# A decoder layer in split fp32: key/value steps two later, one query tile one later, a copy on another engine, last blocks scaled in twos

## The chip, the cores and the metric

The kernel runs on one core of one Trainium2 chip. The metric is the device time of one execution, in microseconds (us). Engines are named as the profile names them: PE is TensorE (PEld its weight loads), DVE is VectorE, ACT is ScalarE, POOL is GpSimd, SP is SyncE, which here only issues DMAs.

## What is computed

One inference step of one layer of a hybrid decoder, in fp32, on 256 prompt positions and 8 sample tokens (264 columns in all) of width 2048:

```python
def trunk_layer(x, attend, shift0, wkv0, lp):
    ...
    x = x + FFN_RES * swiglu(rmsnorm(x, n1), f1g, f1u, f1d)
    h = rmsnorm(x, nm)
    proj = h @ w_in
    ...
    o_att, k_buf, v_buf = attend(q, k, v, sinks)
    o_rwkv, shift, S = rwkv_time_mix(proj[..., ATT_COLS:], shift0, wkv0, mu, w0, w2, a0, a2, g2,
                                     k_k, k_a, r_k, ln_w, ln_b)
    mixed = jnp.concatenate([o_att, o_rwkv.astype(o_att.dtype)], axis=-1)
    x = x + mixed @ w_out
    x = x + FFN_RES * swiglu(rmsnorm(x, n2), f2g, f2u, f2d)
    return x, k_buf, v_buf, S, shift
```

`attend` is attention over a window of 128 positions with sinks and a relative bias (16 query heads in 8 tiles of two, 4 key/value heads in 2 tiles of two); `rwkv_time_mix` is a recurrence with a matrix state for each of 16 heads (8 pairs). A last rmsnorm follows. The new keys, values, states and shift columns are outputs too.

## The kernel before

**Matrix products.** Every weight is read once from memory, in chunks of up to four 128x128 tiles (`raw`, L140, issued by SP). ScalarE casts a chunk to a reduced type (`hi`, L141), and VectorE takes the rest of it (`lo` = raw − hi, through the helper at L68). The activations are split likewise. A product of one tile is three matmuls of 264 columns (hi·hi, hi·lo, lo·hi) through the helper at L84, into an accumulator `acc` in PSUM, of which there are three. A chunk is thus 12 matmuls. In this text they are the projection matmuls, or the big stream.

**Stages.** The first feed-forward part ends near 757 us of the span, mixing (input projection, attention, recurrence, output projection) near 1150, the second feed-forward part near 1921, and the final norm, scaling and stores near 1933.

**Order of work in mixing.** The tiles of the input projection come in the order of `SEQ` (L49). Between the chunks of the projection, everything else is done by generators: after each chunk, `tick` advances each of them by one `yield`, so one step is about one chunk long. `pause(n)` yields n times. They share five PSUM buffers `m`, handed out by `mp()`. A scheduler then sets the final order of the instructions on each engine. The generators are:
- `prep`, once for a pair of recurrent heads. Among other things it transposes (L521, L528), copies the results out (L524 `kr`, L531 and L533 `BT`, the latter two half copies of 64x256 on ScalarE), and does small matmuls XD,ld and uv,gm at L84, whose results ScalarE copies at L544 and L546.
- `chain`, once for each of the four batches of two pairs. It holds the triangular inverse on VectorE (many small `st` and `Xt`), then the tiles `PT`, `kr` and `N` (VectorE, L68), then three state steps: matmuls N,PT and N,kr, then `S` (VectorE, L71), then matmuls S,PT and S,kr, and so on.
- `kvtask`, once for each of two key and two value tiles. It issues the stores out_kp or out_vp from ScalarE's queue (L750) and copies the sample columns into `dkv` on GpSimd (L751), yields once, then transposes dkv (L755) and for value tiles the tile (L758), and copies on ScalarE (L760, L763); L765 stores.
- `attend`, once for each of eight query tiles. Scores (two kv,o tiles, matmuls at L84), addition of the bias and row maximum on VectorE (L801), softmax (exponentials on ScalarE, L78; sums, reciprocal and scaling on VectorE, L68, L776, L75), a pause of `PW[4]` = 9 steps, six transposes (L808 to L810), copies out on ScalarE (L811) and VectorE (L812), then the product with the values (t,kv) and a copy.

**The end.** The last norm's sums and the turning of four of the sixteen output blocks (128x264 each) are done by TensorE (L1045, L1049). The turned part goes out in three stores of 96, 96 and 72 rows: block 0 is scaled on ScalarE and stored by SP (L1066), block 1 is scaled on VectorE and stored by SP (L1069), block 2 is scaled on ScalarE and stored by ScalarE (L1073). Between them ScalarE copies the scale row for GpSimd (L1070). The other twelve blocks are scaled in place and stored by a loop (L1074 to L1078): the first by VectorE and SP, the next three by VectorE and ScalarE's queue, four by GpSimd and SP, four by VectorE and ScalarE's queue.

## Time and profile before

| what | value |
|---|---|
| median of three runs | 1935.79 us (1936.81, 1935.79, 1934.95) |
| profiled execution | 1934.77 us, of it 1932.9 us span |
| mean granted TensorE clock | 0.998 |
| memory read and written | 346.67 MB and 9.69 MB, 184 GB/s over the span |
| ScalarE, VectorE busy | 53%, 68% |

The page of the profile lists how long each engine is busy, the chain of work that ended last, and groups of instructions by line, operation and tile (`out<-in`, shape, count, then busy us and mean ns, then idle time ahead of them and who ended it). The waits of an engine are listed by waiting line and releaser: total us, how many, the longest. A timeline row is start, duration, engine, line, operation, tiles, shape and count; in brackets the idle time ahead and its releaser. On TensorE matmuls overlap, so its pace is read from one start to the next, and not from durations. Times in such rows are us from the start of the span.

### The profile page before, as it was taken

What the parts mean: (1) busy time and instruction counts of PE and PEld (TensorE: products, weight loads), DVE (VectorE), ACT (ScalarE), POOL (GpSimd) and SP (SyncE); (2) the same over time, 40 slices, a digit from 0 to 9 for tenths busy, and PEclk for the clock granted to TensorE, in tenths of its full rate; (3) what the DMA queues carried; (4) which work ended last, traced back from release to release, by engine and by line L of the source; (5) the groups of instructions that cost most, each with busy time, mean ns of one, the idle gap of its engine ahead of it and who ended that gap; (6) DMA issues with size and microseconds to landing.
All of it is one profiled execution on the core that took longest, in us unless ns stands there. A gap on an engine that the chain in (4) does not pass through costs nothing.

```text
span 1932.9 us, 45519 instructions
## 1 busy us (share of the span) xinstructions
PE 1919.4 (99%) x17171; PEld 1897.1 (98%) x17171; DVE 1311.8 (68%) x2606; ACT 1023.7 (53%) x2034; POOL 260.1 (13%) x376
## 2 busy tenths in 40 slices
PE   9999999999999999999999999999999999999998
PEld 9999999999999999999989999999999999999998
DVE  5865555655556568889988977866666666666665
ACT  5644444444444457675657555644444444444446
POOL 0401101011010113222102100300101001010012
PEclk9999999999999999999999999999999999999999
DMA  7666666666666668555646656666666666666664
GB/s 241 178 192 196 185 195 195 183 192 177 190 183 180 188 181 238 177 165 153 176 120 165 210 155 183 175 188 188 189 195 195 186 192 189 194 195 184 193 181 150
DMA packets 218464, 357.27 MB, mean 185 GB/s; under 512 B 33516, under 2 KB 71804, under 8 KB 218244
## 3 DMA queue, kind: packets, MB, share of 16 engines
q1 hardware_dynamic: 211936, 346.02, 60.8%
q10 hardware_dynamic: 6308, 8.35, 1.4%
q8 instruction: 134, 2.20, 0.4%
q14 instruction: 86, 0.70, 0.1%
HBM read 346.67 MB, written 9.69 MB: 184 GB/s over the span
## 4 chain that ended last, share of the span: by engine, by line
PE 96%; DVE 1%; ACT 1%; issue 1%; DMA 0%; POOLq 0%; POOL 0%; ACTq 0%; DVEq 0%
PE acc L84 89%; PE m L84 6%; DVE lo L68 0%; ACT t L78 0%; ACT hi L141 0%; DMA x<-in_x 0%; DVE t L801 0%; DVE st L68 0%; DVE Xt L68 0%; DMA ld<-in_bias 0%; ACT BT L533 0%; ACT L78 0%; POOLq L1187 0%; DVE PT L68 0%; PE m L528 0%
## 5 line engine op out<-in xcount | busy, mean ns | idle before, releaser
L68 DVE TENSOR_TENSOR lo<-raw,hi 128x512 fp32r<-128x512 f32 (+1 forms) x1288 | 874.0, 682 | 510.4 <-ACT hi L141 486.9
L141 ACT CAST hi<-raw 128x512 fp32r<-128x512 f32 (+1 forms) x1288 | 776.8, 606 | 820.2 <-PE acc L84 745.2
L84 PE MATMUL acc<-x,hi 128*128 128x264 f32 x4840 | 893.4, 286 | 0.8 <-ACT hi L141 0.8
L84 PEld LDWEIGHTS acc<-x,hi 128*128 128x128 f32 x4840 | 750.1, 189 | 4.3 <-ACT hi L141 1.0
L84 PE MATMUL acc<-x,lo 128*128 128x264 f32 x2420 | 691.3, 286 | 0.2 <-DVE lo L68 0.2
L84 PE MATMUL acc<-h,hi 128*128 128x264 f32 x2752 | 495.0, 284 | 0.0
L84 PEld LDWEIGHTS acc<-x,lo 128*128 128x128 f32 x2420 | 457.2, 189 | 2.7 <-issue 0.7
L84 PEld LDWEIGHTS acc<-h,hi 128*128 128x128 f32 x2752 | 424.4, 189 | 0.0
L84 PE MATMUL acc<-h,lo 128*128 128x264 f32 x1376 | 387.8, 284 | 0.0
L84 PEld LDWEIGHTS acc<-h,lo 128*128 128x128 f32 x1376 | 259.2, 189 | 0.0
L68 POOL TENSOR_TENSOR t<-t,t 128x264 f32<-128x264 f32 x74 | 79.8, 1078 | 1096.1 <-DVE t L68 949.8
L84 PE MATMUL acc<-y,hi 128*128 128x264 f32 x648 | 122.7, 284 | 0.0
L84 PE MATMUL acc<-o,hi 128*128 128x264 f32 x648 | 120.1, 284 | 0.0
L84 PE MATMUL acc<-kv,hi 128*128 128x264 f32 x582 | 109.8, 285 | 0.0
L84 PEld LDWEIGHTS acc<-y,hi 128*128 128x128 f32 x648 | 101.2, 189 | 0.1
L84 PEld LDWEIGHTS acc<-o,hi 128*128 128x128 f32 x648 | 100.1, 189 | 0.0
L71 DVE SCALAR_TENSOR_TENSOR x<-acc,x 128x264 f32<-128x264 f32 (+1 forms) x193 | 81.1, 425 | 24.3 <-PE acc L84 23.4
L84 PE MATMUL acc<-y,lo 128*128 128x264 f32 x324 | 92.0, 284 | 0.0
L84 PE MATMUL acc<-o,lo 128*128 128x264 f32 x324 | 92.0, 284 | 0.0
L84 PEld LDWEIGHTS acc<-kv,hi 128*128 128x128 f32 x582 | 89.9, 189 | 0.2
L68 DVE TENSOR_TENSOR t<-acc,t 128x264 f32<-128x264 f32 x156 | 67.4, 432 | 32.9 <-PE acc L84 32.9
L84 PE MATMUL acc<-kv,lo 128*128 128x264 f32 x291 | 82.9, 285 | 0.0
(307 smaller groups left out, 1592.5 us busy)
## 6 DMA issues: line engine op xcount, KB each, us to landing
raw<-in_gu SPq DMA_DIRECT2D x688, 256.0 KB, 3.4
raw<-in_dn SPq DMA_DIRECT2D x224, 256.0 KB, 2.9
raw<-in_win SPq DMA_DIRECT2D x152, 256.0 KB, 3.4
raw<-in_dn SPq DMA_DIRECT2D x160, 192.0 KB, 2.8
raw<-in_wout SPq DMA_DIRECT2D x64, 256.0 KB, 3.5
xsp<-x ACTq DMA_DIRECT2D x16, 132.0 KB, 3.4
x<-xsp SPq DMA_DIRECT2D x16, 132.0 KB, 4.2
ld<-in_sT SPq DMA_DIRECT2D x16, 128.0 KB, 3.6
```

The costliest lines, as they stand in the source:

```text
L68: return e.tensor_tensor(out=out, in0=a, in1=b, op=op)
L71: return V.scalar_tensor_tensor(out=out, in0=a, scalar=s, in1=b, op0=op0, op1=op1)
L84: return TE.matmul(out, lhsT, rhs, start=start, stop=stop, **k)
L141: A.copy(hi[:, :w], raw[:, :w])
```

## The change

- Key and value tiles: the one `yield` ahead of the transposes becomes `pause(KVW)` with KVW = 3.
- First query tile (`t` = 0): the pause between softmax and transposes becomes 10 steps instead of 9.
- In the last batch, the second of the two half copies into `BT` runs on VectorE instead of ScalarE (for each of its two pairs).
- The turned block 1 is stored from ScalarE's queue instead of SP's.
- Of the first four blocks of the last loop, SP now stores two and ScalarE's queue two, instead of one and three.

One line is inserted near the top, so line numbers behind L43 are one higher after the change.

```diff
+KVW = 3
...
                 for h in range(2):
-                    A.copy(BT[HALF[h], :, HALF[1]], bp[HALF[1 - h], :, HALF[1]])
+                    (V.tensor_copy if h and bt.i == len(BATCH) - 1 else A.copy)(BT[HALF[h], :, HALF[1]], bp[HALF[1 - h], :, HALF[1]])
...
                     G.tensor_copy(dkv[r, w, p, :], xs[h % len(xs)][r, NP:T])
-                yield
+                yield from pause(KVW)
...
-                yield from pause(PW[4])
+                yield from pause(PW[4] + (not t))
...
                 ts(V, y, x, r, ALU.mult)
-                SP.dma_start(o, y)
+                A.dma_start(o, y)
...
-                for e, q, o, n, r in ((V, SP, 0, 1, rp[:, :T]), (V, A, 1, 3, rp[:, :T]), (G, SP, 4, 4, rb), (V, A, 12, 4, rp[:, :T])):
+                for e, q, o, n, r in ((V, SP, 0, 2, rp[:, :T]), (V, A, 2, 2, rp[:, :T]), (G, SP, 4, 4, rb), (V, A, 12, 4, rp[:, :T])):
```

The scheduler's order moves with it, at more places than the edited ones. In the rows below, names with a number are tiles (the number tells tiles of one name apart), and a count stands at the end.

TensorE around the transposes of the first value tile, in the middle of the input projection (`bk` feeds the `BT` copies, XD,ld and uv,gm are `prep`'s small matmuls). Before, from the transposes of bk, and at the end of the small matmuls:

```order
L84 MATMUL acc_13622<-x_107,hi_13666 128x264 x2
L528 MATMUL m_13334<-C,bk_13035 128x128 x4
L84 MATMUL m_13399<-XD,ld_13268 64x2
...
L84 MATMUL m_13429<-uv_11864,gm_13272 64x64
L755 MATMUL m_13492<-C,dkv 8x128
L758 MATMUL m_13492<-C,t_13370 128x128 x2
```

The same places after:

```order
L529 MATMUL m_13330<-C,bk_13035 128x128 x4
L756 MATMUL m_13366<-C,dkv 8x128
L85 MATMUL acc_13622<-x_107,hi_13666 128x264 x2
L85 MATMUL acc_13622<-x_107,lo_13667 128x264
L85 MATMUL acc_13622<-x_107,hi_13666 128x264
L85 MATMUL m_13399<-XD,ld_13268 64x2
...
L85 MATMUL m_13429<-uv_11864,gm_13272 64x64
L756 MATMUL m_13528<-C,dkv 8x128
L759 MATMUL m_13528<-C,t_13370 128x128 x2
```

A key tile's transpose (m_13366) and projection matmuls now stand between the transposes of bk and the small matmuls; the value tile's transposes still follow the latter.

TensorE around the first query tile's transposes, behind `chain`'s matmuls m_14099 for the second batch. Before:

```order
L84 MATMUL m_14099<-uv_11129,gm_12243 64x64
L808 MATMUL m_14142<-C,t_13690 128x128
L809 MATMUL m_14142<-C,t_13689 128x128
...
L808 MATMUL m_14148<-C,t_13692 128x128
...
L84 MATMUL acc_14157<-x_106,hi_14159 128x264 x2
...
L84 MATMUL m_14176<-N_13888,PT_13393 64x64
```

After:

```order
L85 MATMUL m_14099<-uv_11129,gm_12243 64x64
L85 MATMUL acc_14145<-x_106,hi_14147 128x264 x2
...
L85 MATMUL acc_14145<-x_108,lo_14287 128x264
L85 MATMUL m_14164<-N_13888,PT_13393 64x64
...
L809 MATMUL m_14185<-C,t_13690 128x128
L810 MATMUL m_14185<-C,t_13689 128x128
...
L809 MATMUL m_14191<-C,t_13692 128x128
```

The six transposes have moved behind the matmuls with N; ahead of those stand 18 projection matmuls instead of the transposes and 23.

VectorE at the same place, before:

```order
L68 TENSOR_TENSOR PT_13393<-m_14068,C 64x384
L776 RECIPROCAL stb_14008<-stb_14008 128x4
L68 TENSOR_TENSOR PT_13393<-m_14068,C 64x384
L68 TENSOR_TENSOR kr_11703<-m_14069,kr_11703 128x192
L68 TENSOR_TENSOR lo_14326<-raw_14324,hi_14325 128x512
L68 TENSOR_TENSOR st_14047<-X_13482,Xt_13483 128x64
L68 TENSOR_TENSOR kr_12042<-m_14069,kr_12042 128x192
L75 TENSOR_SCALAR t_13998<-t_13998,stb_14008 128x256
L75 TENSOR_SCALAR t_13999<-t_13999,stb_14008 128x128
L68 TENSOR_TENSOR N_13888<-m_14098,wc 128x512
```

After:

```order
L69 TENSOR_TENSOR PT_13393<-m_14068,C 64x384
L69 TENSOR_TENSOR lo_14326<-raw_14324,hi_14325 128x512
L76 TENSOR_SCALAR t_13998<-t_13998,stb_14008 128x256
L76 TENSOR_SCALAR t_13999<-t_13999,stb_14008 128x128
L69 TENSOR_TENSOR st_14047<-X_13482,Xt_13483 128x64
L69 TENSOR_TENSOR PT_13393<-m_14068,C 64x384
L69 TENSOR_TENSOR kr_11703<-m_14069,kr_11703 128x192
L69 TENSOR_TENSOR kr_12042<-m_14069,kr_12042 128x192
L69 TENSOR_TENSOR N_13888<-m_14098,wc 128x512
```

Between the first PT and N stand the same instructions in another order, without the reciprocal.

## The prediction

> **What bounds the kernel now.** I read the page first: what share of the span each engine is busy, the chain that ended last, and the two costliest groups of the engines beside TensorE.

> ```profile
> span 1932.9 us, 45519 instructions
> ...
> PE 1919.4 (99%) x17171; PEld 1897.1 (98%) x17171; DVE 1311.8 (68%) x2606; ACT 1023.7 (53%) x2034; POOL 260.1 (13%) x376
> ...
> PE 96%; DVE 1%; ACT 1%; issue 1%; DMA 0%; POOLq 0%; POOL 0%; ACTq 0%; DVEq 0%
> ...
> L68 DVE TENSOR_TENSOR lo<-raw,hi 128x512 fp32r<-128x512 f32 (+1 forms) x1288 | 874.0, 682 | 510.4 <-ACT hi L141 486.9
> L141 ACT CAST hi<-raw 128x512 fp32r<-128x512 f32 (+1 forms) x1288 | 776.8, 606 | 820.2 <-PE acc L84 745.2
> ```

> TensorE is the bound: busy for 1919.4 of 1932.9 us. The change takes no matmul away. So it can win only in the 13.5 us in which TensorE is not busy, in the dead time where its two streams meet, and behind its last matmul. Next, TensorE's waits over the whole span, cut to those whose neighbourhood the change moves, and the mixing stage that holds them (columns: stretch, its length, busy PE, PEld, DVE, ACT, POOL, granted clock, DMA share, GB/s):

> ```profile
> PE m L808 <- DVE PT L68: 1.2, 1, 1.2
> ...
> PE m L755 <- issue: 0.7, 1, 0.7
> PE m L84 <- ACT BT L533: 0.4, 1, 0.4
> ...
> PE m L84 <- ACT kr L544: 0.2, 1, 0.2
> ```

> ```profile
> 760.00:1150.00 390.00, 386.97 (x4432) 366.58 (x4431) 334.15 (x924) 246.12 (x627) 68.76 (x167) 1.00 0.58 167
> ```

> These are 2.5 us. In the whole mixing stage TensorE is without work for 390 − 387 = 3.0 us, VectorE is busy for 334 of 390 (86%), and the clock is full. So the ceiling of the three mixing edits is about 3 us plus dead time between streams. Of 1935.79 us, 0.2% is 3.87 us; that is about what a measurement of this kernel can tell from no change. The profiled execution took 1934.77 us (1.9 us lie around its span), 1.0 below the median of the runs: I sum against the profile and carry the difference over to the median.

> **Key and value tiles two steps later.** First TensorE's rows where the transposes of a value tile stood, then ScalarE's:

> ```profile
> 939.05 0.25 PE L84 MATMUL m<-XD,ld 64*64 64x2 f32 x2
> ...
> 940.05 0.27 PE L755 MATMUL m<-C,dkv 128*8 128x128 f32 x1 [0.74 <-issue]
> ```

> ```profile
> 937.08 1.07 ACT L524 COPY kr<-m 64x128 f32<-64x128 f32 x4
> ...
> 939.20 0.74 ACT L533 COPY BT<-m 64x256 f32<-64x256 f32 x2
> ```

> L755 found no free PSUM buffer until ScalarE's L533 copies ended at 939.94; that is the 0.74 us. In the new order the value tile's transposes still stand right behind the XD,ld and uv,gm matmuls, and take a buffer that a small L763 copy (764 now) has freed meanwhile. But the second half of those small matmuls now takes the buffer of the L533 copies. Counted from the four transposes that feed these copies, ScalarE still has by my estimate some half of a cast (0.35 of 0.61, the page's row above) to do, two kr copies (0.54), and the half copies, 0.37 + 0.74: 2.0 us. TensorE has one transpose (0.1), four projection matmuls (0.5) and the first half of the small ones (0.9, an estimate: sixteen uv,gm alone take 0.68 in a row below, and as many XD,ld go between): 1.5. So 0.5 of waiting comes where 0.74 went: −0.25; ends −0.74 (the copies are done in time) and +0.4 (all of their 1.1 us is waited for). The two out_kp/out_vp stores and GpSimd's copies of a kv tile stand ahead of the pause; of the later kvn stores nobody waits.

> **First query tile one step later.** TensorE, then VectorE, where the wait of 1.19 us lies:

> ```profile
> 964.25 0.33 PE L808 MATMUL m<-C,t 128*128 128x128 f32 x1
> ...
> 965.98 0.30 PE L808 MATMUL m<-C,t 128*128 128x128 f32 x1 [1.19 <-DVE PT L68]
> ...
> 966.26 0.49 PE L84 MATMUL acc<-x,hi 128*128 128x264 f32 x2
> 966.59 0.28 PE L84 MATMUL acc<-x,lo 128*128 128x264 f32 x1
> 966.71 0.40 PE L84 MATMUL acc<-x,hi 128*128 128x264 f32 x2
> 966.94 0.28 PE L84 MATMUL acc<-x,lo 128*128 128x264 f32 x1
> ...
> 968.89 0.41 PE L84 MATMUL acc<-x,hi 128*128 128x264 f32 x2
> 969.23 0.27 PE L84 MATMUL m<-N,PT 64*64 64x64 f32 x1
> ```

> ```profile
> 964.61 0.56 DVE L68 TENSOR_TENSOR PT<-m,C 64x384 f32<-64x384 f32 x1
> ...
> 965.28 0.55 DVE L68 TENSOR_TENSOR PT<-m,C 64x384 f32<-64x384 f32 x1
> ...
> 966.14 0.68 DVE L68 TENSOR_TENSOR lo<-raw,hi 128x512 fp32r<-128x512 f32 x1
> ...
> 967.60 0.68 DVE L68 TENSOR_TENSOR N<-m,wc 128x512 f32<-128x512 f32 x1
> ...
> 970.90 0.47 DVE L71 SCALAR_TENSOR_TENSOR S<-m,wc,N 128x64 f32<-128x64 f32 x2
> ...
> 974.24 0.47 DVE L71 SCALAR_TENSOR_TENSOR S<-m,wc,N 128x64 f32<-128x64 f32 x2
> ```

> Before, six transposes come first, the second three wait for the buffer that PT frees, then 23 projection matmuls, then N,PT. After, 18 projection matmuls come first, then N,PT, then the transposes, which wait no more. The pace of projection matmuls is (966.94 − 966.59)/3 = 0.117 us. So TensorE, free at 964.25, reaches N,PT at 964.25 + 18 × 0.117 + 0.2 for two changes of stream = 966.55. VectorE is the one that is late: between the first PT and N the new order has the same instructions, only shuffled (the lo and the softmax scalings now ahead of the second PT) and without the reciprocal that lay between the two PT (some 0.1 us). So N ends near 967.60 + 0.68 − 0.1 = 968.2: **a new wait of 1.6 us at N,PT takes the place of the 1.19**. Behind N,PT still come the six transposes (twice 966.26 − 965.98, 0.56), five projection matmuls (0.6) and 0.1 of changing, so the place that was reached at 969.23 is reached at 969.45: +0.2. The next state step S has two lo ahead of it instead of one (+0.68) and lacks two copies: VectorE is there at about 970.8, TensorE at 971.5, no wait. The second S follows 3.3 us later on VectorE (974.24 − 970.90), so ends near 974.5, 3.0 after TensorE's 971.5. TensorE has 7 projection matmuls (0.8), the kv,o block (1.16, by a row quoted for the next edit), the t,kv block, which is no longer, and two changes of stream in between, 2.4 to 3.3 us: it waits 0 to 0.6 us, I take 0.2. Together +0.4; ends −1.35 (from 964.63, where the first three transposes have been fed, to 965.98: all of it is won) and +1.5.

> **A key copy on VectorE.** The last batch's half copies, the wait there, and the prices:

> ```profile
> 1058.38 0.68 PE L84 MATMUL m<-uv,gm 64*64 64x64 f32 x16
> 1059.50 1.16 PE L84 MATMUL m<-kv,o 64*128 64x256 f32 x6 [0.44 <-ACT BT L533]
> ```

> ```profile
> 1058.70 0.74 ACT L533 COPY BT<-m 64x256 f32<-64x256 f32 x2
> ...
> 1059.54 0.38 ACT L544 COPY kr<-m 128x256 f32<-128x256 f32 x1
> ```

> ```profile
> L533 ACT COPY BT<-m 64x256 f32<-64x256 f32 x16 | 5.9, 367 | 0.2
> ...
> L812 DVE COPY t<-m 128x128 f32<-128x128 f32 x16 | 4.2, 281 | 0.7 <-ACT t L811 0.7
> ...
> L636 DVE COPY uv<-m 64x512 f32<-64x512 f32 x4 | 2.7, 684 | 0.8 <-ACT uv L636 0.7
> ```

> ScalarE loses 2 × 0.367 us; VectorE gains two copies of 256 columns, between 0.281 (128) and 0.684 (512), by the line through both 0.415 each, 0.83. [...] Nobody is behind them at once: VectorE is not the bound there. In the new order the first of TensorE's two kv,o tiles waits for ScalarE's kr copy (L544) and the second, nine projection matmuls on, for the VectorE copy. ScalarE, packed here, gets to L544 up to 0.74 earlier, 1059.92 becoming 1059.2; TensorE, with three projection matmuls fewer ahead, is there 0.36 earlier, near 1058.7. So 0.5 us of waiting is left of 0.64 (0.44 here and 0.2 for the kr copy, in the waits above): −0.15; ends −0.64 (gone) and +0.3 (VectorE's copy late).

> **Dead time between streams.** A pair of projection matmuls takes 0.23 us in the stream, but 966.59 − 966.26 = 0.33 right behind small ones, and 969.23 − 968.89 = 0.34 right ahead of them: a visit to the small stream costs 0.2. Counted in the two orders, visits fall from 104 to 100: −0.8 at most, 0 at least where waits cover them; I take −0.6.

> **The tail.** VectorE's scalings, SyncE's second store, ScalarE's last issues, and two stretches behind the last matmul:

> ```profile
> 1924.20 2.47 DVE L68 TENSOR_TENSOR y<-y,m 128x264 f32<-128x264 f32 x3
> ...
> 1924.58 0.42 SPq L1069 DMA_DIRECT2D out_yt<-yt  x1
> ...
> 1925.61 1.44 ACTq L1078 DMA_DIRECT2D out_yT<-y  x2
> ```

> ```profile
> 1925.00:1926.00 1.00, 0.00 (x0) 0.00 (x0) 1.00 (x2) 0.21 (x1) 1.00 (x1) 0.89 0.95 281
> ...
> 1929.00:1930.00 1.00, 0.00 (x0) 0.00 (x0) 0.00 (x0) 0.00 (x0) 0.00 (x0) 0.50 1.01 413
> ```

> VectorE scales the same eight blocks in the same three instructions, so the last four are ready when they were, and the two last stores issue when they did. From 1925 on the 16 DMA engines are full (0.95 to 1.01) to near the end: bytes, not issues, set the finish. What can be won is a larger first piece (264 KB instead of 132) a little earlier; ScalarE's 72-row piece waits behind the moved store instead. −0.15; ends −0.5 and +0.4 (the moved store's issue ahead of ScalarE's ACTIVATE). [...]

> **Sum.** −0.25 + 0.4 − 0.15 − 0.6 − 0.15 = −0.75: 1934.0 for the profiled execution, **1935.0** against the median.

> **Rivals.** *All three waits vanish and none follows*: −0.74 − 1.35 − 0.64 − 0.8 − 0.15 = −3.7, 1932.1. For it: each wait is single and its cause is moved away. Against: VectorE is 86% busy, and N is not earlier. *Slower*: VectorE's queue stalls on ScalarE's casts. The new order has four lo (one before the second PT, two before the first S, one before the second) on the path to N and S; each that finds its cast unfinished stops everything behind it, for 0.38 (486.9/1288, the mean) to 0.61 us (a cast). Four cost 1.5 to 2.4 us, net +0.75 to +1.65: 1937.4 at the worst, slower from 0.75 us of such stalls on, and past 0.2% only if two more batches pay the like (+1.65 + 2 × 2.4 = +6.45, 1942). For it: VectorE's mixing load; against: before, the same lo waited there for nothing. *Nothing is gained*: waits only move, 1935.8.

> **Chances.** Forecast 0.55, all vanish 0.17, slower 0.13, nothing gained 0.15. All five terms at their best ends make 1935.0 − 0.5 − 1.75 − 0.5 − 0.2 − 0.35 = 1931.7, all at their worst + 0.65 + 1.1 + 0.45 + 0.6 + 0.55 = 1938.4; the medians themselves are good to some ±0.5 (the three runs lie within ±0.9). I give 1931.5 to 1937.5: the worst ends do not come together, and the slower rival's 1937.4 is just inside. Faster by over 0.2% (below 1931.9) needs the first rival and the tail's best end: 0.08; slower by over 0.2% needs the second in several batches: 0.05; within it 0.87.

> **What would show it.** Right: no wait of L756 (755 before), a wait of 1 to 2 us of TensorE on VectorE's N, no wait of L809 on PT, ScalarE's last store issued as far behind its first scaling as before, and the DMA share as full behind it. Wrong: TensorE without any wait of over 0.5 us in mixing (first rival), VectorE idle for hi between PT and S (second), or a difference of over 2 us outside mixing and tail, of which I have no term.

## The result, and the profile after

| | median of runs | lowest to highest | runs |
|---|---|---|---|
| before | 1935.50 us | 1934.83 to 1937.71 | 8 |
| after | 1941.39 us | 1937.63 to 1943.72 | 8 |

The ratio, estimated over all runs and not from the medians alone (they would give 1.0030), is 1.0025, 95% interval 1.0015 to 1.0035: slower, with the whole interval above 1. The forecast was 1935.0 us, between 1931.5 and 1937.5. Also new is the spread: six microseconds over the runs of after, three over those of before.

The profiled execution of after took 1942.33 us, with 1940.5 us span, 7.6 more than before. Its page has TensorE as busy as before by share, yet for longer (1923.9 us instead of 1919.4), with the same 17171 matmuls:

```profile
span 1940.5 us, 45520 instructions
...
PE 1923.9 (99%) x17171; PEld 1900.8 (98%) x17171; DVE 1315.2 (68%) x2608; ACT 1024.2 (53%) x2032; POOL 258.7 (13%) x376
```

TensorE's waits over the span of after (waiting line, releaser, total, how many, longest):

```profile
PE m L85 <- ACT kr L545: 2.2, 2, 2.0
PE m L85 <- DMA ld<-in_kc: 1.6, 1, 1.6
PE m L85 <- DVE N L69: 1.1, 1, 1.1
PE acc L85 <- ACT hi L142: 1.0, 1, 1.0
PE m L85 <- POOL eps L169: 1.0, 1, 1.0
PE m L85 <- ACT BT L534: 0.7, 1, 0.7
```

The waits on L808 and L755 are gone, those on N and BT have come in their place, as forecast. The first two rows were not forecast: a wait of 2.0 us for a copy of ScalarE, and one of 1.6 us for a load of sample keys. All listed waits together grew from 4.7 to 7.8 us. That is 3.1 of 7.6 us. The rest is in TensorE's clock. Stretches around the two long waits, with the granted clock in the third column from the right:

```profile
982.00:984.00 2.00, 0.44 (x11) 0.35 (x9) 1.19 (x4) 1.72 (x6) 0.19 (x1) 0.87 0.58 148
984.00:990.00 6.00, 6.00 (x32) 5.98 (x31) 5.59 (x19) 5.66 (x17) 0.19 (x1) 0.50 0.46 130
990.00:992.00 2.00, 2.00 (x16) 1.48 (x15) 0.90 (x3) 1.06 (x3) 0.00 (x0) 0.92 0.68 190
1061.00:1065.00 4.00, 2.09 (x72) 1.87 (x66) 2.05 (x7) 3.92 (x17) 0.14 (x1) 1.00 0.52 181
1065.00:1069.00 4.00, 3.89 (x16) 3.06 (x17) 1.80 (x5) 1.70 (x6) 1.58 (x6) 0.57 0.81 197
```

From 983.5 to 990.3 the clock is halved: the whole of 984 to 990, and by the mean clock 0.5 us of the stretch ahead (0.87 over 2 us) and 0.3 of the one behind. That is 6.8 us. Behind the second wait it is halved for 3.4 us (0.57 over 4 us). Together 10.2 us at half speed cost 5.1 us, an estimate that takes TensorE as the bound throughout them. The same 6 us in before, for comparison, with 49 matmuls instead of 32:

```profile
984.00:990.00 6.00, 6.00 (x49) 5.47 (x49) 5.11 (x16) 4.41 (x12) 0.19 (x1) 1.00 0.48 118
```

So 5.1 us of clock and 3.1 of waits make 8.2, with a remainder of −0.6 to the 7.6. Over the runs the spread follows the clock too: the run of 1937.63 us has a mean granted clock of 0.999, those of 1938.98 and 1939.14 have 0.998, 1941.05 has 0.997, 1941.73 to 1942.33 have 0.996, 1943.72 has 0.995. A thousandth of 1940 us is 1.9 us. The fastest run lies 2.8 us above the fastest of before, at a mean clock of 0.999: about what the waits grew by. The median lies 3.8 us above the fastest run, and in before 0.7; so some 3.1 of the median's 5.9 us are put down to the clock.

**Where the two waits come from.** Both are read on the engine that releases them. First SP's issues of sample key loads, before, and then after:

```profile
976.00 1.00 SPq L378 DMA_DIRECT2D ld<-in_kc  x2
```

```profile
978.31 0.33 SPq L379 DMA_DIRECT2D ld<-in_kc  x1
979.93 0.33 SPq L379 DMA_DIRECT2D ld<-in_kc  x1
```

And VectorE ahead of the last of these in after:

```profile
977.52 0.48 DVE L802 CUSTOM_DVE_ANT_0 t<-m,ld,vec 128x256 f32<-128x256 f32 x1
...
978.20 0.43 DVE L69 TENSOR_TENSOR pj<-acc,rs 128x264 f32<-128x264 f32 x1
978.54 0.68 DVE L69 TENSOR_TENSOR lo<-raw,hi 128x512 fp32r<-128x512 f32 x1
979.14 0.48 DVE L802 CUSTOM_DVE_ANT_0 t<-m,ld,vec 128x256 f32<-128x256 f32 x1
...
979.54 0.35 DVE L802 CUSTOM_DVE_ANT_0 t<-m,ld,vec 128x128 f32<-128x128 f32 x1
```

Sample keys and bias tiles share six `ld` buffers. In the new order pj and lo stand between the two score tiles of a query (before, the four L801 stood together), so the second bias tile is read until 979.9. That is 0.9 us of the delay; the rest is that VectorE comes to its first score tile 2.3 us later than before (977.52 against 975.22), while TensorE comes to its key matmuls only 1.8 us later (981.22 against 979.46). SP can issue the last key load only then, it lands 3.68 us later (the chain of waits has it from 979.93), and TensorE has tiny matmuls and then nothing until 983.65.

Second, ScalarE ahead of the kr copy that TensorE awaits until 1065.11:

```profile
1061.07 0.51 ACT L79 ACTIVATE t<-t,sta 128x256 f32<-128x256 f32 x1
...
1062.84 0.47 ACT L79 ACTIVATE stc<-sta,vec 128x2 f32<-128x2 f32 x2
1063.21 0.60 ACT L142 CAST hi<-raw 128x512 fp32r<-128x512 f32 x1
1063.84 0.37 ACT L532 COPY BT<-m 128x256 f32<-128x256 f32 x1
1064.22 0.37 ACT L534 COPY BT<-m 64x256 f32<-64x256 f32 x1
1064.62 0.17 ACT L547 COPY XD<-m 128x8 f32<-128x8 f32 x1
1064.68 0.38 ACT L545 COPY kr<-m 128x256 f32<-128x256 f32 x1
```

The exponentials of a query tile, 2.2 us with what belongs to them, stand ahead of these copies, with one cast between. Before, they stood ahead of them too, but were over at 1057.5, 1.6 us before TensorE was done with the small matmuls ahead of its kv,o tile (1059.06). Now they are over at 1063.3, and TensorE has been waiting at kv,o since 1063.09.

### The profile page after: what moved, and what is told of

It is laid out like the page before. It is cut to its first block, busy times and chain, and to the rows that moved or that the text cites. A ratio compares the mean times of both kernels' runs of the same rounds, so it can differ in the third digit from the quotient of the medians.

```text
span 1940.5 us, 45520 instructions
## 1 busy us (share of the span) xinstructions
PE 1923.9 (99%) x17171; PEld 1900.8 (98%) x17171; DVE 1315.2 (68%) x2608; ACT 1024.2 (53%) x2032; POOL 258.7 (13%) x376
## 4 chain that ended last, share of the span: by engine, by line
PE 96%; DVE 1%; ACT 1%; issue 1%; DMA 0%; POOLq 0%; POOL 0%; ACTq 0%; DVEq 0%
PE acc L85 89%; PE m L85 6%; ACT t L79 0%; DVE t L802 0%; DMA x<-in_xT 0%; DVE lo L69 0%; DMA ld<-in_kc 0%; ACT hi L142 0%; ACT BT L534 0%; ACT kr L525 0%; DVE Xt L69 0%; PE m L529 0%; DVE st L69 0%; POOLq L1188 0%; PE m L809 0%
```

## The experiments

**Theory A:** the first query tile's step makes both long waits, through the order on VectorE and ScalarE, and idle time of TensorE in turn halves its clock. **Theory B:** the half copy on VectorE frees its buffer too late. **C:** the key/value steps shift the later softmax. **D, E, F:** the clock has nothing to do with the waits, or the wait at kv,o does not matter, or the clock falls because of what runs, not because TensorE idles. Medians stand beside the median of before on the same chip.

### Which edit it is

The query tile's step alone:

```diff
-                yield from pause(PW[4])
+                yield from pause(PW[4] + (not t))
```

> Only the first query tile's extra step is made. Theory A (this edit alone brings the two new long waits of TensorE, on the sample key loads and on ScalarE's kr copy behind the exponentials, and the clock is halved for some 3.4 us or twice that behind them): 3 to 6 us slower than before, the profile with at least one stretch of granted clock 0.5 in mixing and a wait on ld<-in_kc of over 1 us. Theory B (the half copy on VectorE frees its buffer too late): within 1 us of before, no such stretch.

Measured: 1940.41 us against 1935.52, ratio 1.0023 [1.0014, 1.0032]. Its waits, the two long ones first:

```profile
PE m L84 <- DMA ld<-in_kc: 1.7, 1, 1.7
PE m L84 <- ACT BT L533: 1.7, 1, 1.7
```

and the clock behind the second:

```profile
1063.00:1067.00 4.00, 4.00 (x21) 4.00 (x21) 2.85 (x13) 2.10 (x8) 1.40 (x5) 0.57 0.80 198
```

This one edit alone loses 4.9 us of the 5.9. In its profile (mean granted clock 0.997) only the second wait was followed by a halved stretch; its runs go from 1937.26 (clock 0.999) to 1944.40 (0.995).

The key/value steps alone (KVW = 3):

> Only the key and value tiles' two steps are made. Theory A: no long wait, no halved clock in mixing, 0 to 1 us faster than before. Theory B: the same. If the kv steps are what shifts the softmax of the last batches (theory C): 3 us or more slower, with a wait of over 1 us in mixing.

Measured: 1936.07 us, 1.0005 [0.9996, 1.0014]. No halved clock in mixing in its profile (mean granted clock 0.998, as in that of before); the wait on L809 is still there with 1.4 us, and BT takes 1.2 us in two waits. No gain, no loss that can be told.

The half copy on VectorE alone:

> Only the last batch's half copy goes to VectorE. Theory A: within 1 us of before, the wait on BT at the last kv,o gone or shorter, no halved clock in mixing. Theory B: 2 to 5 us slower, with a wait of over 1 us at the last pair's kv,o.

Measured: 1936.32 us, 1.0003 [0.9994, 1.0012], no halved clock in mixing in its profile (mean 0.998), though its wait on PT is 2.1 us there. Theory B falls. (In the profile of after the copy takes 0.42 us on VectorE; the prediction had 0.415 from the line through two rows.)

The whole change without the query tile's step:

> The whole change without the first query tile's extra step. Theory A: 0.5 to 2 us faster than before (1933.5 to 1935 against 1935.5), no halved clock in mixing. Theory B: 2 to 5 us slower than before, because the half copy on VectorE is still there.

Measured: 1937.58 us, 1.0011 [1.0002, 1.0020]. No halved clock in mixing in its profile (mean 0.999), as theory A has it, but 2.1 us slower than before, where theory A had it faster: the other edits together make a wait of 1.2 us on kr, and the listed waits sum to 6.6 us instead of 4.7. The edits are not additive; each moves the order of the rest.

The two edits of the tail alone; all ahead of them keeps its order:

> Only the two edits at the end (turned store on ScalarE's queue, blocks in twos); all before them keeps its order. The prediction's term: -0.15 us (-0.5 to +0.4) behind the last matmul, the DMA share as full. If what is left of the change without the query tile's step (2.1 us slower with the other three edits) comes from the tail: +0.5 to +1.5.

Measured: 1935.41 us against 1935.87, 0.9998 [0.9990, 1.0007]. The term was small, and the tail has no part in the loss.

### Whether idle time is what halves the clock

Eight waits in the densest stretch of the kernel before, the down projection of the second feed-forward part, in three lengths (n = 0, 3 and 6):

```diff
+        def gap():
+            m1, m2, z = mp(), mp(), tmp((P, P))
+            behind(mm(m1[:, :P], ones, ones))
+            with tc.high_priority():
+                V.tensor_copy(z, m1[:, :P])
+                for _ in range(n):
+                    ts(V, z, z, 1.0, ALU.mult)
+            big[0] = mm(m2[:, :P], z, ones)
```

> The kernel before with eight short waits put into TensorE's densest stretch, the down projection of the second feed-forward part: a 128-column matmul, one VectorE copy of it, a matmul of the copy, then the next tile. By rows of like copies each wait is 0.7 to 1.2 us, eight are 6 to 10 us. Theory A with a bound for the idle time near 1.5 us: no halved clock, the kernel is longer by the sum of the waits alone. If any wait of this size can halve the clock: up to 1.7 us more for each.

> The kernel before with eight waits in the down projection as in the two kernels above, with three VectorE operations in each: 1.8 to 2.2 us. Theory A: between the 0.83 us waits, none of which halved the clock, and the 2.74 us waits, of which five of eight did; the length over the short-wait kernel is 8 times the difference of the waits (8 to 11 us) plus 1.7 us for each halved stretch, 0 to 4 of them.

> The same with six more VectorE operations in each wait, 2.2 to 3.2 us each, eight are 18 to 26 us. Theory A: most of the waits are followed by a stretch of 3.4 us at half clock, which costs 1.7 us more each, so the kernel is longer by the sum of the waits plus 5 to 14 us. Theory D: by the sum of the waits alone.

TensorE's waits of the three, shortest first (the expectation of n = 3 puts the waits of the other two at 0.83 and 2.74 us; as the profile lists them they are 0.6 and 2.5 on average):

```profile
PE m L84 <- DVE t L149: 4.5, 8, 0.6
```

```profile
PE m L84 <- DVE t L75: 13.5, 8, 1.7
```

```profile
PE m L84 <- DVE t L75: 19.9, 8, 2.6
```

Medians 1947.07 against 1935.30, 1954.89 against 1936.25 and 1968.29 against 1935.30 us; ratios 1.0057 [1.0044, 1.0071], 1.0098 [1.0084, 1.0112] and 1.0170 [1.0155, 1.0186]. So 11.8 us are paid for 4.5 of waits, 18.6 for 13.5 and 33.0 for 19.9. Over the waits that is 7.3, 5.1 and 13.1. All three pay for sixteen added matmuls and the breaks in the stream; the profile of the first also has a halved stretch near the start of the kernel (shown at the end), some 1.7 of its 7.3. The third pays 7 to 8 us more than the other two. In its profile (mean granted clock 0.994) five of the eight waits are followed by a halved stretch of 3.4 us (five times 1.7 is 8.5); in the profiles of the other two (0.998 both) no wait is. One of the five, matmuls around a wait that ends at 1433.5:

```profile
1433.53 0.80 PE L84 MATMUL m<-ones,t 128*128 128x128 f32 x2 [2.47 <-DVE t L75]
1433.98 0.79 PE L84 MATMUL acc<-h,hi 128*128 128x264 f32 x2
1434.57 0.42 PE L84 MATMUL acc<-h,lo 128*128 128x264 f32 x1
1434.79 0.64 PE L84 MATMUL acc<-h,hi 128*128 128x264 f32 x2
...
1437.20 0.41 PE L84 MATMUL acc<-h,hi 128*128 128x264 f32 x2
1437.45 0.30 PE L84 MATMUL acc<-h,lo 128*128 128x264 f32 x1
```

A matmul of 264 columns every 0.22 us, then again every 0.12. The three kernels differ only in the length of the waits, so here the longer wait alone brought the halved clock: eight waits of 1.7 us drew none, five of eight of 2.5 us drew one. Why five of eight like waits: within one trace the edges of the halved stretches lie whole multiples of 3.41 us apart (983.49, 990.31, 1065.41 and 1068.82 in after; 1065.41 − 983.49 is 24 of them). In windows of 3.41 us counted from such an edge, a wait may lie within one window or across two. Of the eight waits of n = 6, here the window with the most work that was followed by a halved stretch, and the one with the least that was not:

```profile
1689.49:1692.90 3.41, 1.14 (x10) 0.94 (x8) 2.83 (x10) 0.88 (x2) 0.00 (x0) 1.00 0.58 190
1406.18:1409.59 3.41, 1.52 (x13) 1.33 (x12) 2.90 (x9) 1.13 (x2) 0.00 (x0) 1.00 0.81 253
```

Where TensorE was idle for 2.3 us of a window, the next window came at half clock; where it was idle for 1.9 us, at full clock.

### The same in the changed kernel

Seven `ld` buffers instead of six, run twice:

> The changed kernel with seven buffers instead of six for the small loads, so that the last sample key load need not wait for a bias tile to be read by VectorE; TensorE's order is the same up to there. Theory A: the wait on ld<-in_kc and the halved clock behind it go, the wait on kr of the last batch stays: 2.5 to 5 us faster than the changed kernel (1936.5 to 1939). Theory D (the clock has nothing to do with the waits; it falls by chance or by load): only the 1.6 us of the wait go, halved stretches in mixing stay as frequent.

> The changed kernel with seven small-load buffers once more, as the comparison on the same chip: 1939 to 1942 by both theories, runs spread over 5 us or more.

Measured: 1941.55 us against 1935.30 and 1941.43 against 1936.25; ratios 1.0028 [1.0017, 1.0040] and 1.0025 [1.0016, 1.0035]. The wait on the key load is gone, and so is the halved stretch behind it; but the time is not better than that of after, against theory A's number. Most of the 1.6 us came back in other waits: all listed waits together are 7.2 and 7.0 us in the two profiles, against 7.8. In the first of these profiles the clock is halved behind the remaining wait on kr for 10.2 us instead of 3.4, and once more near the start of the kernel (0.52 from 8 to 11 us). Why that wait draws longer stretches there was not settled.

The key load's wait filled with work whose result is not used:

```diff
+                        if p == 0 and b == 4 and j == 2:
+                            for _ in range(4):
+                                tc.keep_in_program_order(mm(sps[:, 128:128 + T], ident, la))
```

> The changed kernel with four idle fp32 matmuls of 264 columns (their result is not used) put on TensorE just where it waits for the last sample key load, some 1.8 us of work in a wait of 1.6. Theory A (the clock falls because TensorE idles): added work does not lengthen the kernel; no halved clock behind the key load, 1 to 4 us faster than the changed kernel. Theory D, or a loss by the waits alone: 0 to 1 us slower than the changed kernel, halved stretches as before.

Measured: 1939.87 us against 1935.30, 1.0023 [1.0013, 1.0032]; 1.5 us under the median of after, which was not measured beside it, no halved clock in its profile up to the last matmul (mean granted clock 0.999). The order behind it moved as well (the wait on kr is 1.3 us in it), and its interval overlaps that of after, so this alone decides little.

The cleaner pair: the other wait filled, in the kernel with seven buffers.

```diff
+                if bt.i == len(BATCH) - 1 and k:
+                    for _ in range(4):
+                        tc.keep_in_program_order(mm(dps[:, 64:64 + T], ident, la))
                 A.copy(KR[:, 2], gv[:, :256].rearrange("p (c t) -> p c t", c=4))
```

> The changed kernel with seven small-load buffers (the key load's wait is gone in it) and four idle fp32 matmuls of 264 columns on TensorE just ahead of the kv,o tile that waits 2.0 us; their result is not used. Theory A (TensorE's idle time lowers the clock): the wait is filled with some 1.8 us of work, halved stretches there go, 1.5 to 4 us faster than the same kernel without the four matmuls on the same chip, and the runs lie closer together. Rival F (the clock falls because of what runs there, not because TensorE idles): 0 to 1 us slower than without them, as many halved stretches.

Measured: a median of 1939.39 us against 1941.43 without the four matmuls, on the same chip: 2.0 us lower with more work. The means are only 1.1 us apart, and the intervals against before (1.0011 to 1.0029, 1.0016 to 1.0035) overlap, so the time alone does not settle it. The clock does more: the mean granted clock is 0.998 in eight of its eleven runs, and in two of the ten without. The four take 2.05 us in its profile, from 1058.48 on, and of the wait 0.8 us is left. The stretch at kv,o and the one behind it, without the four (the clock falls to half):

```profile
1059.00:1063.00 4.00, 1.99 (x13) 1.45 (x12) 2.24 (x8) 3.48 (x14) 0.84 (x4) 0.99 0.68 187
1063.00:1069.00 6.00, 6.00 (x27) 5.36 (x27) 3.36 (x13) 1.79 (x4) 1.19 (x4) 0.50 0.87 244
```

and with them (it stays):

```profile
1058.00:1062.00 4.00, 3.17 (x40) 2.21 (x34) 2.07 (x7) 3.94 (x16) 0.35 (x2) 1.00 0.55 178
1062.00:1066.00 4.00, 4.00 (x31) 3.69 (x31) 2.05 (x11) 1.49 (x5) 0.53 (x4) 1.00 0.86 207
```

Theory D falls with this and the three lengths of waits above. Rival F falls in its plain form: what ran there is still there. But dense matmuls went in where the idle time was, so the pair does not tell idle time from too little work; of the next runs one profile speaks for the latter in mixing (a halved stretch behind a wait of 0.7 us).

The kr copy on VectorE, in the changed kernel, there with seven buffers, and in the kernel before:

```diff
-                A.copy(KR[:, 2], gv[:, :256].rearrange("p (c t) -> p c t", c=4))
+                (V.tensor_copy if bt.i == len(BATCH) - 1 else A.copy)(KR[:, 2], gv[:, :256].rearrange("p (c t) -> p c t", c=4))
```

> The changed kernel with the last batch's kr copy (the one that the 2.0 us wait at kv,o is put down to) on VectorE instead of ScalarE, where it stood behind the exponentials and two half copies; TensorE's order differs in 17 rows. Theory A (the long waits cost their length, and some of them a halved clock behind them): that wait falls to about 0.8 us, halved stretches behind it become rare, 1 to 3.5 us faster than the changed kernel. Theory E (the wait at kv,o and the clock behind it are not what the change costs): within 0.5 us of the changed kernel.

> The same with seven small-load buffers as well, so both long waits are shortened. Theory A: the fastest of the runs within 1.5 us of the fastest of before, no or one halved stretch in most runs, median 1936 to 1938. Theory E: 1940 to 1942.

> The kernel before with the last batch's kr copy on VectorE, nothing else of the change. Theory A: the waits of 0.44 and 0.2 us at the last kv,o go or shrink, 0 to 0.6 us faster than before, if nothing is late in their place; no halved clock in mixing.

Measured: 1940.89, 1938.84 and 1935.98 us against 1935.87 (1.0025 [1.0015, 1.0036], 1.0017 [1.0008, 1.0026], 1.0002 [0.9993, 1.0011]). The first is a miss: the wait hardly shrank, it only changed its releaser, because on VectorE the copy stands behind a softmax sum that itself needs the last exponential.

```profile
PE m L85 <- DVE kr L545: 1.8, 1, 1.8
PE m L85 <- DMA ld<-in_kc: 1.6, 1, 1.6
```

So this did not test E as meant. Its profile has a halved stretch behind this wait, none behind the 1.6 us of the key load (an edge falls inside that wait, near 984.3 by 13 × 3.41 from 939.92), and one in a place where the only wait is the 0.7 us on BT, amid matmuls of 2 and 64 columns:

```profile
936.51:939.92 3.41, 2.73 (x102) 2.49 (x101) 3.17 (x13) 2.69 (x8) 0.25 (x1) 1.00 0.58 166
939.92:943.34 3.42, 3.42 (x18) 3.42 (x18) 2.23 (x8) 1.67 (x7) 1.11 (x6) 0.50 0.79 255
```

With both measures (seven buffers too) the median comes 2.6 us under that of after, but not to the 1936 to 1938 of theory A; its fastest run (1937.13) lies 2.3 above the fastest of before. No version tried beats the kernel before by more than can be told; nearest is the tail alone.

## Why the prediction was wrong

- **Key and value tiles: the place was right, the size a little off.** The new wait on BT stands where it was forecast, at the second half of the small matmuls, with 0.7 us instead of 0.5. It replaces 0.74: the term was near 0 instead of −0.25, and the edit alone measured 1.0005.
- **First query tile: the right wait up to N, and then cut off.** The wait on N came, 1.1 us instead of 1.6, and the wait on PT went. Two errors nearly cancel in the 1.6, which is luck: 27 projection matmuls stand ahead of N,PT in the profile of after (965.04 to 968.4), not 18, so TensorE comes some 1.1 us later than worked out, and VectorE came to its first PT 0.7 us later. The state steps had no wait, against 0.2. But there the working stopped. The score tiles behind them moved too, pj and lo slipped in between on VectorE, and with them moved the freeing of the `ld` buffers that SP's key loads stand waiting for. The prediction did not follow the step to SP's queue; +0.4 was forecast, 1.6 us of wait and a halved clock came.
- **Key copy on VectorE: the failing step is "ScalarE, packed here, gets to L544 up to 0.74 earlier".** That took ScalarE's times from before. In the new order the exponentials ahead of the copies are still running when TensorE comes, and ScalarE gets to the kr copy 2.0 us after TensorE is there, not 0.5. The query tile's step does this alone (1.7 us, on BT).
- **Dead time between streams** was not tried by itself. The remainder of −0.6 us in the profiled pair is as large as the term, but it holds every other difference too, so it does not show it.
- **The tail**: −0.15 forecast, 0.9998 measured. ScalarE's last issue ends 2.6 us behind the last matmul before and 2.7 after, SP's 2.8 and 2.8, and the DMA engines were as full: a share of 0.95 to 1.05 in the five microseconds from 1925 on before, 0.96 to 1.05 in those from 1933 on after. A term of −0.15 is too small to be told from 0 by these runs.
- **The missing term.** "The clock is full" was read from before as a property of the stage. In these runs it hung on the waits: the sum counted a wait at its length, while behind those of 1.6 and 2.0 us in the profile of after came 6.8 and 3.4 us of halved clock, by estimate 1.7 us on top for each 3.4. Of the median's 5.9 us some 3.1 are this term. The other 2.8, the waits, would by themselves put the median near 1938.3, which is outside the range too. None of the rivals had either: the slower one had VectorE waiting for casts, which did not happen.

All signs that the prediction named for being right came, and none of those for being wrong. They lay at the places of the edits, and what cost the time came some 14 and 95 us behind the wait on N.

The halved stretches in the profiles are 3.4, 6.8 and 10.2 us long, and by the mean granted clock (0.995 to 0.999 in the eight runs of after) runs of the same kernel draw none or several. The longest wait of TensorE in the lists is 2.6 us (n = 6). In a dense stretch 2.3 us of idle time in one window were enough, in mixing waits of 1.6 to 2.0 us, and once 0.7 us amid tiny matmuls.

## What to carry to other kernels

When one step of a planned order moves, read the new order of every engine that frees what TensorE needs, loads included, to the end of the stage; a release computed from the old order is a guess. Where TensorE is nearly always busy, look at the longest single wait as well as at the sum: the eight waits of 1.7 us in the dense stretch drew no halved clock, and of those of 2.5 us five cost by estimate some 1.7 us more each through it. A stretch of tiny matmuls deserves the same look even where the waits in it are shorter (0.7 us in one profile here). A wide spread of the runs that follows the mean granted clock (here 1937.6 us at 0.999 to 1943.7 at 0.995) was the sign of it, and work thrown into the wait helped to tell.

## What the runs showed of the hardware that was not expected

```profile
8.00:11.00 3.00, 3.00 (x16) 3.00 (x15) 2.67 (x5) 1.81 (x4) 0.00 (x0) 0.50 1.02 393
```

```profile
8.00:11.00 3.00, 3.00 (x27) 3.00 (x26) 2.41 (x4) 1.53 (x3) 0.00 (x0) 1.00 0.99 382
```

The runs of before fall into two groups, 1934.8 to 1935.6 and 1936.4 to 1936.8 in one set of fifteen, 1.5 us apart; such a stretch at the start, 1.7 us by the same estimate, would make that difference, though no profile of a slower one of these runs was taken.
